# Stick-breaking scores copied to SBUF by ScalarE, and attention steps taken at one point of a weight chunk where there were two

## The chip, the cores and the metric

One NeuronCore of a Trainium2 chip runs the whole kernel. The metric is the device time of one execution in microseconds. TensorE is called PE here, its weight loads PEld, VectorE DVE, ScalarE ACT, GpSimd POOL, and the queue that issues the transfers SP.

## The reference, cut to what matters

One decoder layer over 512 tokens of width 2048. After an RMSNorm, one projection `w_in` gives the inputs of two groups of 16 heads of width 64. Group A is sliding-window attention (window 128) with four key/value heads, normalised queries and keys, a relative bias and a sink per head. Group B is stick-breaking attention, and it is this group's arithmetic that the change touches:

```python
z = jnp.einsum('bhqd,bhsd->bhqs', q_blk, kt) * scale          # scores
log_beta = jax.nn.log_sigmoid(z)
log_1m = jnp.where(causal, jax.nn.log_sigmoid(-z), 0.0)
later = lax.cumsum(log_1m, axis=3, reverse=True) - log_1m
w = jnp.where(causal, jnp.exp(log_beta + later), 0.0)         # causal: key before query
out = jnp.einsum('bhqs,bhsd->bqhd', w, vt)
```

With sp(z) = log(1 + exp(z)), the exponent is z minus the sum of sp over the keys from s up to the query. Both groups' outputs are normalised, go through one projection `w_out`, and are added to x; a squared-ReLU MLP of width 8192 follows.

## The kernel before, in words

**Projections.** All products keep float32 precision by three matmuls on split operands (a high part `hi` and a remainder `lo`). `wchunk` (L95) loads a piece of weights, 2 x 128 rows of 512 columns, and splits it: ACT casts it to `hi` (L91), DVE subtracts to get `lo` (L92). The loaded pieces have four buffers (`wst`), the `hi` and `lo` tiles four each (`whl`). A group of 512 projected columns takes 8 such chunks. A chunk is 24 matmuls of 128x512 for four accumulators `m` (or `t`) of PSUM, six for each. The groups follow one another: keys and values of A, two groups of queries of A (`qa`), values of B (`v0`), two groups of queries and keys of B (`qk0`, `qk1`), `v1`, `qk2`, `qk3`, and then the output projection of A's half (`out_group(0, n)`, four times four chunks).

**Attention inside the projections.** Attention has no stage of its own. Its steps are interleaved with the projections' chunks by `pump` (L283), which is called twice in every chunk: after the second accumulator (the middle) and after the fourth (the end). The unit of work is a piece of a pair of heads: two units (`hf`) for each of 8 pairs of A, four units (`i`, one for each block of 128 queries) for each of 8 pairs of B, 48 units in all. A unit has a `begin` and an `end`. `begin` computes the scores (tile `sc` in A, `z` in B, two PSUM banks, one for each head) and the long chain of small operations behind them. `end` transposes the finished weights on PE (tile `ptr` in A, `wtr` in B, two banks), DVE copies the transposes to SBUF (`turned`, `wt`); the last unit of a pair (in A, of two pairs) also multiplies them with the values (`av`, `bv`) and passes the result to `finish_o` (L377).

**The order by `pump`.** Its calls are counted by `clock`. On an odd call, the middle of a chunk, the next unit begins if one is due (`LAG` = 11 calls after it was enqueued). On an even call, the end of a chunk, the unit before the one that has just begun ends. The `end` of a unit therefore comes one and a half chunks after its `begin`. A `None` in the queue `flight` marks a call in which nothing began, so that the last unit can end too. The generators in `chains` (the norms of A's queries and keys) are advanced on each call. A unit's two score banks, two transpose banks and the output bank all come from the pool `pa`, which has four banks (`bank`, L86); the other four (`pp`) hold the projection's accumulators.

**The chain of a unit of B** (`weights`, L562) for each of its two heads, on 128 x w elements with w = 128, 256, 384 or 512: ACT takes the absolute value of `z` (L571), its exponential (L572) and logarithm (L573) in tile `a`; DVE adds max(z, 0) into tile `b` (L574); POOL zeroes the diagonal block's upper part (L575); DVE sums from the right with a scan into `a` (L578); DVE subtracts `a` from `z` into `b` (L580); POOL masks (L581); ACT takes the exponential (L583). L571, L574 and L580 read `z` in PSUM. Tiles `a` and `b` come from the pool `wk` with two buffers for each tag.

Instructions run in order on each engine. The framework places each engine's instructions by the order in the program and by readiness in its own model, so that a few matmuls of a projection may stand between two steps of attention.

Of the kernel before, what the change touches and what calls it, by code (L numbers as in the profile page):

```python
# [15 lines left out]
ALU = mybir.AluOpType  # L16
# [4 lines left out]
P = 128  # L21
# [37 lines left out]
def hymba_layer(ctx: ExitStack, tc: tile.TileContext, x, norm_attn_g, w_in, q_norm_g, k_norm_g,  # L59
                sinks, rel_bias, swa_out_g, sb_out_g, w_out, norm_mlp_g, w_up, w_down, sel, eye, out):  # L60
    nc = tc.nc
    x, out = x[0], out[0]
# [211 lines left out]

    chains, units, flight, clock = [], deque(), deque(), [0]

    def enqueue(pair_units):
# [3 lines left out]
    def pump():  # L283
        clock[0] += 1
        chains[:] = [g for g in chains if next(g, None) is not None]
        if clock[0] % 2:
            begun = bool(units) and units[0][0] <= clock[0]
            if begun:
                begin, end = units.popleft()[1]
                begin()  # L290
                flight.append(end)
            flight.append(None) if not begun and flight else None
        elif len(flight) > 1:
            end = flight.popleft()
            if flight[0] is None:
                flight.clear()
            end()

    def drain():
        while units or flight:  # L300
# [124 lines left out]
    def swa_pair(g, m, q, turned):  # L425
        c = 4 * g + m
        k = kT[g]
        heads = (8 * g + m, 8 * g + m + 4)
        bias = []

        def load_bias():
            bias.append(wk.tile([P, 2, 2 * P], F32, tag="bias", bufs=4, name=f"bias{c}"))

            with tc.issue_after(last_in[0].ins):
                for s in range(2):
                    nc.sync.dma_start(out=bias[0][:, s], in_=bias_ap(heads[s]))
        prs_of = {}

        def scores(hf):
            sc = [bank(f"sc{c}_{hf}{s}") for s in range(2)]  # L440
            for nn in range(2):
                n = 2 * hf + nn
                k0 = max(n - 1, 0) * P
                o0 = nn * 256 if n else P
                for a, b in ((0, 0), (0, 1), (1, 0)):
                    for s in range(2):
                        rows = slice(s * DH, (s + 1) * DH)
                        nc.tensor.matmul(sc[s][:, o0:o0 + 256], q[rows, a, n * P:(n + 1) * P],
                                         k[rows, b, k0:k0 + 256],
                                         start=(a == 0 and b == 0), stop=(a == 1))  # L450
            return sc

        def softmax(hf, sc):
            prs = []
            bt = bias[0]
            for s in range(2):
                h = heads[s]
                pr = wk.tile([P, 2, 256], F32, tag=("wa", "wb")[s], name=f"pr{c}_{hf}{s}")
                scv = sc[s].rearrange("p (n k) -> p n k", n=2)
                if hf == 0:  # L460
                    nc.gpsimd.memset(pr[:, 0, 0:P], NEG)
                    nc.vector.tensor_tensor(out=pr[:, 0, P:], in0=scv[:, 0, P:], in1=bt[:, s, P:], op=ALU.add)
                    nc.vector.tensor_tensor(out=pr[:, 1], in0=scv[:, 1], in1=bt[:, s], op=ALU.add)
                else:
                    nc.vector.tensor_tensor(out=pr, in0=scv,
                                            in1=bt[:, s:s + 1].broadcast_to([P, 2, 256]), op=ALU.add)
                mx = sm.tile([P, 2], F32, tag="mx", name=f"mx{c}_{hf}{s}")
                nc.vector.tensor_reduce(out=mx, in_=pr, axis=AX.X, op=ALU.max)
                nm = sm.tile([P, 2], F32, tag="nm", name=f"nm{c}_{hf}{s}")
                nc.vector.tensor_scalar(out=nm, in0=mx, scalar1=sink[:, h:h + 1], scalar2=-1.0,  # L470
                                        op0=ALU.max, op1=ALU.mult)
                den = sm.tile([P, 2], F32, tag="den", name=f"den{c}_{hf}{s}")
                es = sm.tile([P, 2], F32, tag="es", name=f"es{c}_{hf}{s}")
                for nn in range(2):
                    nc.scalar.activation(out=pr[:, nn], in_=pr[:, nn], func=AF.Exp, bias=nm[:, nn:nn + 1],
                                         accum_out=den[:, nn:nn + 1])
                nc.scalar.activation(out=es, in_=nm, func=AF.Exp, bias=sink[:, h:h + 1])
                nc.vector.tensor_tensor(out=den, in0=den, in1=es, op=ALU.add)
                nc.vector.reciprocal(out=den, in_=den)
                for nn in range(2):  # L480
                    nc.gpsimd.tensor_scalar(out=pr[:, nn], in0=pr[:, nn], scalar1=den[:, nn:nn + 1],
                                            scalar2=1.0, op0=ALU.mult, op1=ALU.mult)
                prs.append(pr)
            return prs

        def turn(hf, prs):
            b0 = 1 if hf == 0 else 0
            f0 = 0 if hf == 0 else 3 * P
            for s in range(2):
                tr = bank(f"ptr{c}_{hf}{s}")  # L490
                prf = prs[s].rearrange("p n k -> p (n k)")
                for b in range(b0, 4):
                    nc.tensor.transpose(tr[:, b * P:(b + 1) * P], prf[:, b * P:(b + 1) * P], ident)
                nc.vector.tensor_copy(out=turned[m][:, s, f0:f0 + (4 - b0) * P], in_=tr[:, b0 * P:])

        def begin(hf):
            if hf == 0:
                load_bias()
            prs_of[hf] = softmax(hf, scores(hf))

        def end(hf):
            if hf == 0:
                turned[m] = wtp.tile([P, 2, 7 * P], F32, tag="wt", name=f"pt{c}")
            turn(hf, prs_of.pop(hf))
            if hf == 0 or m % 2 == 0:
                return

            for s in range(2):
                kv = slice((2 * g + s) * DH, (2 * g + s + 1) * DH)
                av = bank(f"av{c}_{s}")  # L510
                for j in (0, 2, 1, 3):
                    n = min(256, T - j * P)
                    for r in range(2):
                        nc.tensor.matmul(av[r * DH:(r + 1) * DH, j * P:j * P + n], va[j][:, kv],
                                         turned[m - 1 + r][:, s, j * 256:j * 256 + n],
                                         start=(j == 0), stop=(j == 3))
                finish_o(av, 0, 4 * g + 2 * s + m // 2)

        return [(partial(begin, hf), partial(end, hf)) for hf in range(2)]
# [29 lines left out]
    def sb_pair(c, q, k, vs, keep):  # L549
# [12 lines left out]
        def weights(i, sc):  # L562
            w = (i + 1) * P
            dg = slice(i * P, (i + 1) * P)
            ws = []
            for s in range(2):
                z = sc[s][:, 0:w]
                a = wk.tile([P, 512], F32, tag=("wa", "wc")[s], name=f"a{c}_{i}{s}")[:, 0:w]
                b = wk.tile([P, 512], F32, tag=("wb", "wd")[s], name=f"b{c}_{i}{s}")[:, 0:w]

                nc.scalar.activation(out=a, in_=z, func=AF.Abs)  # L571
                nc.scalar.activation(out=a, in_=a, func=AF.Exp, scale=-1.0)  # L572
                nc.scalar.activation(out=a, in_=a, func=AF.Ln, bias=1.0)  # L573
                nc.vector.scalar_tensor_tensor(out=b, in0=z, scalar=0.0, in1=a, op0=ALU.max, op1=ALU.add)  # L574
                nc.gpsimd.affine_select(out=b[:, dg], in_=b[:, dg], pattern=[[-1, P]], compare_op=ALU.is_gt,  # L575
                                        fill=0.0, base=0, channel_multiplier=1)

                nc.vector.tensor_tensor_scan(out=a[:, ::-1], data0=ones2[:, 0:1].broadcast_to([P, w]),  # L578
                                             data1=b[:, ::-1], initial=0.0, op0=ALU.mult, op1=ALU.add)
                nc.vector.tensor_tensor(out=b, in0=z, in1=a, op=ALU.subtract)  # L580
                nc.gpsimd.affine_select(out=b[:, dg], in_=b[:, dg], pattern=[[-1, P]], compare_op=ALU.is_gt,  # L581
                                        fill=NEG, base=0, channel_multiplier=1)
                nc.scalar.activation(out=b, in_=b, func=AF.Exp)  # L583
                ws.append(b)
            return ws
# [13 lines left out]
        def end(i):  # L599
            if i == 0:  # L600
                wt.extend(wtp.tile([P, 4, 512], F32, tag="wt", name=f"wt{c}_{s}") for s in range(2))
            turn(i, ws_of.pop(i))
            if i < 3:
                return
            av = bank(f"bv{c}")
            cc = c % 4
            for j in range(4):
# [454 lines left out]
    for cj in range(2 * NC):  # L1062
# [8 lines left out]
        for s, (name, ai, _, b, more) in enumerate(d_products(cj)):  # L1071
# [36 lines left out]
            a = act[c, ai]  # L1108

            at_end = q == 14 * NC - 1  # L1110
            for h, tt in sorted(((h, tt) for h in range(2) for tt in range(2)), key=lambda x: x[::-1] if at_end else x):
# [3 lines left out]
                for kk in range(2):  # L1115
                    al, ar = a[:, 0, 2 * h + kk, ts], a[:, 1, 2 * h + kk, ts]
                    first, end = h == 0 and kk == 0 and not more, h == 1 and kk == 1
# [36 lines left out]
```

## Time and profile before

| what | us |
|---|---|
| median of 3 runs (1998.0 to 1998.86) | 1998.21 |
| the profiled execution's own time | 1998.97 |
| span of its trace, first to last instruction | 1997.2 |
| PE busy in it | 1976.4 |
| DVE busy in it | 1649.4 |
| ACT busy in it | 1037.5 |
| POOL busy in it | 1011.3 |

Matmuls are pipelined and a recorded matmul overlaps the next, so PE's busy time is close to the span almost everywhere and says little about lost time. The distance between the starts of two neighbouring projection matmuls says more: whatever stands between them shows as a longer distance. Attention of A lies between about 139 and 280 us of the span, that of B between 319 and 455 us (pairs 0 to 3) and 494 and 629 us (pairs 4 to 7).

### The profile page before, as it was taken

To read this page: it belongs to the slowest core of one execution; us is meant where nothing else is said; L and a number is where in the kernel's file an instruction comes from. 1 tells how busy PE (TensorE), PEld (TensorE's weight loads), DVE (VectorE), ACT (ScalarE), POOL (GpSimd) and SP (SyncE) were. 2 spreads that over 40 slices of the span, in tenths; PEclk is the share of its full clock that TensorE was granted. 3 is DMA by queue.
4 is the path that set the end of the run, shared out by engine and by line. 5 is a ranking of instruction groups with operands and counts; after the bars stand their busy time and mean duration, and the time that the engine had idled before them with its cause. 6 is when DMAs were issued, how large, how long until landed. Compare 5 with 4: busy or idle time off the path is not lost.

```text
span 1997.2 us, 31358 instructions
## 1 busy us (share of the span) xinstructions
PE 1976.4 (99%) x11652; PEld 1717.5 (86%) x11652; DVE 1649.4 (83%) x2142; ACT 1037.5 (52%) x1900; POOL 1011.3 (51%) x898
## 2 busy tenths in 40 slices
PE   8999999999999999999999999999999999999999
PEld 7887787778777889999999999998888888888887
DVE  4469654664776479999999999999999999999997
ACT  6357544453554575656565656565443333333444
POOL 0013431221321038777777777776866656656653
PEclk9999999999999999999999999999999999999999
DMA  6732332224245555665656565656766457456451
GB/s 224 146 119 80 100 98 83 75 69 137 93 140 172 192 169 180 217 201 189 208 181 215 180 216 181 212 176 245 290 250 250 158 221 291 161 221 261 143 204 67
DMA packets 213916, 350.31 MB, mean 175 GB/s; under 512 B 9779, under 2 KB 154372, under 8 KB 206596
## 3 DMA queue, kind: packets, MB, share of 16 engines
q1 hardware_dynamic: 211216, 345.02, 51.0%
q10 hardware_dynamic: 2548, 3.30, 1.3%
q8 instruction: 91, 1.49, 0.3%
q14 instruction: 61, 0.50, 0.1%
HBM read 270.16 MB, written 78.12 MB: 174 GB/s over the span
## 4 chain that ended last, share of the span: by engine, by line
PE 89%; DVE 5%; ACT 3%; POOL 1%; issue 1%; DMA 1%; POOLq 0%; SPq 0%; DVEq 0%; ACTq 0%
PE ps_u L831 11%; PE ps_u L830 11%; PE ps_u L832 11%; PE ps_d L1119 9%; PE ps_d L1120 9%; PE ps_d L1118 9%; PE ps_qk L123 3%; PE ps_qk L125 3%; PE ps_qk L124 3%; PE ps_o L125 2%; PE ps_o L123 2%; PE ps_o L124 2%; PE ps_qa L123 1%; PE ps_qa L124 1%; PE ps_qa L125 1%; DVE lo_d L92 1%
## 5 line engine op out<-in xcount | busy, mean ns | idle before, releaser
L832 PE MATMUL ps_u<-h2h,lo_u 128*128 128x256 f32 x1792 | 507.5, 283 | 0.1
L830 PE MATMUL ps_u<-h2h,hi_u 128*128 128x256 f32 x1792 | 507.6, 283 | 0.0
L831 PE MATMUL ps_u<-h2l,hi_u 128*128 128x256 f32 x1792 | 507.4, 283 | 0.0
L1118 PE MATMUL ps_d<-hi_d,ad 128*128 128x512 f32 x896 | 348.8, 389 | 2.7 <-ACT e L856 2.7
L1119 PE MATMUL ps_d<-lo_d,ad 128*128 128x512 f32 x896 | 349.0, 390 | 0.1
L1120 PE MATMUL ps_d<-hi_d,ad 128*128 128x512 f32 x896 | 348.7, 389 | 0.0
L832 PEld LDWEIGHTS ps_u<-h2h,lo_u 128*128 128x128 f32 x1792 | 344.1, 192 | 0.3 <-DVE lo_u L92 0.3
L831 PEld LDWEIGHTS ps_u<-h2l,hi_u 128*128 128x128 f32 x1792 | 344.2, 192 | 0.0
L830 PEld LDWEIGHTS ps_u<-h2h,hi_u 128*128 128x128 f32 x1792 | 344.1, 192 | 0.0
L806 POOL TENSOR_TENSOR s_u<-st_u 128x256 f32<-128x256 f32 x256 | 212.1, 849 | 245.1 <-DVE lo_u L92 176.3
L965 POOL TENSOR_TENSOR T<-st_d,T 128x1024 f32<-128x1024 f32 x64 | 174.2, 2724 | 188.3 <-DVE lo_d L92 185.8
L92 DVE TENSOR_TENSOR lo_d<-T,hi_d 128x1024 fp32r<-128x1024 f32 x128 | 250.5, 1971 | 19.5 <-ACT hi_d L91 18.9
L92 DVE TENSOR_TENSOR lo_u<-s_u,hi_u 128x512 fp32r<-128x512 f32 x256 | 261.8, 1023 | 0.3 <-ACT hi_u L91 0.3
L91 ACT CAST hi_u<-st_u 128x384 fp32r<-128x384 f32 x256 | 131.2, 513 | 229.4 <-PE ps_u L831 224.1
L91 ACT CAST hi_d<-T 128x1024 fp32r<-128x1024 f32 x128 | 134.9, 1055 | 188.5 <-PE ps_d L1120 175.6
L92 DVE TENSOR_TENSOR lo_u<-st_u,hi_u 128x384 fp32r<-128x384 f32 x256 | 196.1, 766 | 30.4 <-ACT hi_u L91 29.5
L1118 PEld LDWEIGHTS ps_d<-hi_d,ad 128*128 128x128 f32 x896 | 168.2, 188 | 38.0 <-ACT e L856 3.1
L1119 PEld LDWEIGHTS ps_d<-lo_d,ad 128*128 128x128 f32 x896 | 168.2, 188 | 36.1 <-DVE lo_d L92 1.3
L1120 PEld LDWEIGHTS ps_d<-hi_d,ad 128*128 128x128 f32 x896 | 168.2, 188 | 34.8
L92 DVE TENSOR_TENSOR lo_d<-st_d,hi_d 128x1024 fp32r<-128x1024 f32 x96 | 189.7, 1988 | 9.1 <-ACT hi_d L91 9.0
L91 ACT CAST hi_d<-st_d 128x1024 fp32r<-128x1024 f32 x96 | 101.3, 1056 | 154.3 <-PE ps_d L1120 135.4
L91 ACT CAST hi_u<-s_u 128x512 fp32r<-128x512 f32 x256 | 158.5, 619 | 18.0 <-POOL s_u L806 18.0
(242 smaller groups left out, 3818.9 us busy)
## 6 DMA issues: line engine op xcount, KB each, us to landing
st_u<-in_w_up SPq DMA_DIRECT2D x128, 512.0 KB, 3.7
st_d<-in_w_down SPq DMA_DIRECT2D x64, 1024.0 KB, 8.3
ad<-ac SPq DMA_DIRECT2D x56, 1024.0 KB, 6.3
ac<-ah SPq DMA_DIRECT2D x32, 896.0 KB, 4.0
ac<-al SPq DMA_DIRECT2D x32, 896.0 KB, 5.8
st_qk<-in_w_in SPq DMA_DIRECT2D x64, 256.0 KB, 3.0
st_o<-in_w_out SPq DMA_DIRECT2D x32, 512.0 KB, 4.2
st_qa<-in_w_in SPq DMA_DIRECT2D x16, 512.0 KB, 4.0
```

What stands on the lines that cost most here:

```text
L91: cast = nc.scalar.copy(out=hi, in_=st)
L92: nc.vector.tensor_tensor(out=lo, in0=st, in1=hi.bitcast(F32), op=ALU.subtract)
L123: nc.tensor.matmul(ps, ah, bh, start=first, stop=False)
L124: nc.tensor.matmul(ps, ah, bl, start=False, stop=False)
L806: last_sum[0] = nc.gpsimd.tensor_tensor(out=o, in0=a, in1=b, op=op)
L830: nc.tensor.matmul(o, wh[:, a], hh[:, b], start=first, stop=False, skip_group_check=True)
L831: nc.tensor.matmul(o, wh[:, a], hl[:, b], start=False, stop=False, skip_group_check=True)
L832: nc.tensor.matmul(o, wl[:, a], hh[:, b], start=False, stop=(k == KP - 1), skip_group_check=True)
L965: nc.gpsimd.tensor_tensor(out=o, in0=raw[cj, a, h], in1=raw[cj, b, h], op=ALU.subtract)
L1118: nc.tensor.matmul(o, al, bh[:, kk], start=first, stop=False, skip_group_check=True)
L1119: nc.tensor.matmul(o, al, bl[:, kk], start=False, stop=False, skip_group_check=True)
L1120: nc.tensor.matmul(o, ar, bh[:, kk], start=False, stop=end, skip_group_check=True)
```

## The change

In `weights`, ACT first copies the scores `z` to tile `b` in SBUF; the sum with max(z, 0), the mask and the scan then work in place in tile `a`, and the last subtraction takes the scores from `b`. In `pump`, the `end` of a unit moves from the end of a chunk to the middle of the next one, in front of the `begin` that stands there; its product with the values is split off as `values` and comes behind that `begin`. The marker `None` goes. Even calls now only advance `chains`.

```diff
         if clock[0] % 2:
             begun = bool(units) and units[0][0] <= clock[0]
+            values = flight.popleft()() if len(flight) > 1 or flight and not begun else None
             if begun:
                 begin, end = units.popleft()[1]
                 begin()
                 flight.append(end)
-            flight.append(None) if not begun and flight else None
-        elif len(flight) > 1:
-            end = flight.popleft()
-            if flight[0] is None:
-                flight.clear()
-            end()
+            if values:
+                values()
...
             turn(hf, prs_of.pop(hf))
-            if hf == 0 or m % 2 == 0:
-                return
+            return values if hf and m % 2 else None
+
+        def values():
...
+                nc.scalar.copy(out=b, in_=z)
 
                 nc.scalar.activation(out=a, in_=z, func=AF.Abs)
                 nc.scalar.activation(out=a, in_=a, func=AF.Exp, scale=-1.0)
                 nc.scalar.activation(out=a, in_=a, func=AF.Ln, bias=1.0)
-                nc.vector.scalar_tensor_tensor(out=b, in0=z, scalar=0.0, in1=a, op0=ALU.max, op1=ALU.add)
-                nc.gpsimd.affine_select(out=b[:, dg], in_=b[:, dg], pattern=[[-1, P]], compare_op=ALU.is_gt,
+                nc.vector.scalar_tensor_tensor(out=a, in0=z, scalar=0.0, in1=a, op0=ALU.max, op1=ALU.add)
+                nc.gpsimd.affine_select(out=a[:, dg], in_=a[:, dg], pattern=[[-1, P]], compare_op=ALU.is_gt,
                                         fill=0.0, base=0, channel_multiplier=1)
 
                 nc.vector.tensor_tensor_scan(out=a[:, ::-1], data0=ones2[:, 0:1].broadcast_to([P, w]),
-                                             data1=b[:, ::-1], initial=0.0, op0=ALU.mult, op1=ALU.add)
-                nc.vector.tensor_tensor(out=b, in0=z, in1=a, op=ALU.subtract)
+                                             data1=a[:, ::-1], initial=0.0, op0=ALU.mult, op1=ALU.add)
+                nc.vector.tensor_tensor(out=b, in0=b, in1=a, op=ALU.subtract)
...
             turn(i, ws_of.pop(i))
-            if i < 3:
-                return
+            return values if i == 3 else None
+
+        def values():
```

## Rows read from the trace of the kernel before

**Rows 1.** The page: the chain that ended last, shares of the span by engine.

```profile
PE 89%; DVE 5%; ACT 3%; POOL 1%; issue 1%; DMA 1%; POOLq 0%; SPq 0%; DVEq 0%; ACTq 0%
```

**Rows 2.** Windows: start:end, length, PE, PEld, DVE, ACT, POOL busy, clock, DMA.

```profile
319.00:455.00 136.00, 132.38 (x648) 98.99 (x647) 89.18 (x150) 73.72 (x161) 33.77 (x70) 0.99 0.25 73
455.00:494.00 39.00, 39.00 (x174) 32.28 (x173) 15.19 (x16) 13.19 (x17) 7.32 (x5) 1.00 0.44 138
```

**Rows 3.** Waits of PEld, 130 to 660 us: total us, times, longest.

```profile
PEld z L558 <- DVE b L580: 9.8, 18, 1.1
PEld bv L609 <- DVE wt L593: 6.2, 16, 0.5
...
PEld wtr L592 <- ACT b L583: 1.5, 2, 1.0
```

**Rows 4.** Timeline of PE at narrow scores: start us, us; brackets: idle before.

```profile
361.86 0.39 PE L125 MATMUL ps_v<-hi_v,hT 128*128 128x512 f32 x1
...
362.73 0.51 PE L123 MATMUL ps_v<-hi_v,hT 128*128 128x512 f32 x1
363.07 0.40 PE L124 MATMUL ps_v<-lo_v,hT 128*128 128x512 f32 x1
...
382.58 0.39 PE L125 MATMUL ps_v<-hi_v,hT 128*128 128x512 f32 x1
383.61 1.21 PE L558 MATMUL z<-hl_b,hl_b 64*128 64x256 f32 x6 [0.64 <-DVE b L580]
384.75 0.50 PE L123 MATMUL ps_v<-hi_v,hT 128*128 128x512 f32 x1
...
588.69 0.39 PE L125 MATMUL ps_o<-hi_o,ohl 128*128 128x512 f32 x1
...
590.77 0.50 PE L123 MATMUL ps_o<-hi_o,ohl 128*128 128x512 f32 x1
```

**Rows 5.** Timeline of PE, matmuls around the 512-wide scores.

```profile
339.63 0.39 PE L125 MATMUL ps_v<-hi_v,hT 128*128 128x512 f32 x1
...
343.27 0.79 PE L123 MATMUL ps_v<-hi_v,hT 128*128 128x512 f32 x1
...
375.21 0.39 PE L125 MATMUL ps_v<-hi_v,hT 128*128 128x512 f32 x1
...
376.55 0.50 PE L123 MATMUL ps_v<-hi_v,hT 128*128 128x512 f32 x1
...
514.14 0.39 PE L125 MATMUL ps_o<-hi_o,ohl 128*128 128x512 f32 x1
...
517.22 0.50 PE L123 MATMUL ps_o<-hi_o,ohl 128*128 128x512 f32 x1
```

**Rows 6.** Window behind the first of those scores, columns as in rows 2.

```profile
344.00:348.00 4.00, 4.00 (x19) 3.26 (x18) 0.93 (x2) 2.94 (x6) 1.57 (x2) 0.79 0.48 135
```

**Rows 7.** Timeline of PE around a unit's eight transposes.

```profile
387.37 0.40 PE L125 MATMUL ps_v<-hi_v,hT 128*128 128x512 f32 x1
387.61 1.04 PE L592 MATMUL wtr<-ident,b 128*128 128x128 f32 x8
388.40 0.48 PE L123 MATMUL ps_v<-hi_v,hT 128*128 128x512 f32 x1
```

**Rows 8.** Timeline of DVE, the chain of a 512-wide unit.

```profile
379.21 1.29 DVE L574 SCALAR_TENSOR_TENSOR b<-z,a 128x512 f32<-128x512 f32 x2 [1.80 <-ACT a L573]
...
382.89 1.26 DVE L580 TENSOR_TENSOR b<-z,a 128x512 f32<-128x512 f32 x2
```

**Rows 9.** Timeline of ACT, the same unit.

```profile
376.54 1.09 ACT L571 ACTIVATE a<-z 128x512 f32<-128x512 f32 x2
...
384.70 0.62 ACT L583 ACTIVATE b<-b 128x512 f32<-128x512 f32 x1
```

**Rows 10.** Tile z: count, min/median/max ns, first and last start.

```profile
L571 ACT ACTIVATE a<-z x64: 257/432/599, 320.9 to 615.7; 128x128 f32<-128x128 f32 x16, 128x256 f32<-128x256 f32 x16, 128x384 f32<-128x384 f32 x16, 128x512 f32<-128x512 f32 x16
```

**Rows 11.** Timeline of POOL, the same unit's first masks.

```profile
380.03 0.29 POOL L575 TENSOR_SCALAR_AFFINE_SELECT b<-b 128x128 f32<-128x128 f32 x1 [4.00 <-DVE b L574]
380.63 1.09 POOL L575 TENSOR_SCALAR_AFFINE_SELECT b<-b 128x128 f32<-128x128 f32 x1 [0.30 <-DVE b L574]
```

## The prediction

> **What bounds the kernel now.** I read the chain that ended last first: it runs through PE for 89% of the span [rows 1], so the time is PE's work plus what PE waits for. The change touches only the stretch in which attention is interleaved with projections, so next come the windows of that stretch. Without attention PE places 173 or 174 matmuls in 39.00 us, one every 0.23 us. In the first stretch of group B the same matmuls share 136 us with attention, and there DVE is busy for 89.18 us and ACT for 73.72 us [rows 2]. Neither of the two is full; ACT has some 62 us to spare. PE is the bound in this stretch too, and the question is only which waits stand in its queue.
>
> The list of what the weight loads waited for answers that. The scores of B wait 9.8 us for the subtraction L580, the product with the values 6.2 us for the copies of the transposes, and the transposes 1.5 us for the last exponential [rows 3]. A weight load runs ahead of its matmul, so part of each wait is hidden. The true price is seen in the distance between the projection matmuls on both sides. Around a narrow score that waits for nothing it is 362.73 - 361.86 = 0.87 us. Around the score that follows a 512-wide unit it is 384.75 - 382.58 = 2.17 us and, at the last such place, 590.77 - 588.69 = 2.08 us [rows 4]. There are four such places, each 1.2 to 1.3 us too long. The releaser in the row is L580 because a score needs two of the four banks, and the unit before still holds its two until L580 has read `z`.
>
> Around a 512-wide score that waits for nothing the distance is 376.55 - 375.21 = 1.34 us. At the first pair of each half of B it is 343.27 - 339.63 = 3.64 us and 517.22 - 514.14 = 3.08 us [rows 5], 2.30 and 1.74 us too long. After the first of these PE's granted clock averages 0.79 over 4 us [rows 6], which loses another 0.21 x 4 = 0.84 us: between its two levels of 2.4 and 1.2 GHz it spent part of the window at the lower, after PE had stood idle.
>
> **The change part by part.**
>
> *The bank is given back earlier.* `z` is now read last by L574. For a 512-wide unit L574 ends at 380.50 us where L580 ends at 384.15 us [rows 8], 3.65 us earlier. The two copies come in front and cost as much as the two absolute values of the same size, 1.09 us [rows 9]. So the banks come free about 2.6 us earlier, at 381.6 us, while the next score was wanted soon after 382.58 us [rows 4]; now it has the transposes of another unit in front of it as well, which for a 512-wide unit take 388.40 - 387.37 - 0.23 = 0.80 us [rows 7]. The four waits go: 4 x 1.25 = **-5.0 us**, all of it PE's own time.
>
> *The first wide score of each half.* Here DVE and ACT also evacuate the projected queries and keys, and everything is late. The same 2.6 us stand against 2.30 and 1.74 us, so both could go, with the low clock: -4.88 us at most. But ACT has 4 copies more in just these chunks. If one of the two waits stays, -1.7 remains. I take **-4.0**.
>
> *Transposes half a chunk later.* The end of a unit moves by 12 matmuls, 2.8 us; the chain gets 1.09 us longer. The 1.5 us of waits for the last exponential go: **-1.5** (bounds -1.5 and 0).
>
> *Values behind the next score.* The copies of the transposes used to be covered by what the framework put in between; now a score stands there, at least 0.64 us of PE work (0.87 - 0.23). The 6.2 us are the upper bound, 0 the lower, since some waits may be hidden already and DVE can be at a cast when the transposes end. I take **-2.0**, nearer to the lower end because a score is shorter than the two copies.
>
> *Fewer interruptions.* The matmul behind a score is followed at 363.07 - 362.73 = 0.34 us in place of 0.23 [rows 4], so a return to the projection costs 0.11. Transposes and scores now come together in all 48 units: up to 48 x 0.11 = 5.3 us less, or nothing if the step from transposes to scores costs the same. I take **-1.0**.
>
> *Added work on ACT.* 64 copies from PSUM, sizes as in L571, 64 x 432 ns = 27.6 us [rows 10] over the two stretches of B, 14 us each against some 62 us free in the first [rows 2]. Queued behind them on ACT are the casts of weights, for which DVE's `lo` and then PE wait; with four buffers those run chunks ahead, and no projection matmul stands in the list of waits for them. Priced at nothing for that cover. If it were gone, every copy would be PE's loss, 27.6 us.
>
> *Latency of the chain.* This is the point to watch, since transposes that come too early block everything behind them on PE. For the wide unit the scores start at 375.44 us (375.21 + 0.23) and the last exponential ends at 385.32 [rows 5, 9], 9.9 us; with the copies 11.0. After the change the transposes come 48 matmuls (11.0 us), two scores (1.11 + 0.64) and one set of transposes (at most 0.80) later: 13 to 13.5 us. Two and more us of room. Against this speaks POOL: its first mask takes 0.29 us and the second 1.09 us [rows 11], which ends only as the first head's scan on DVE does. The subtraction now has both inputs in SBUF, so it may do the same to a mask: at most 0.7 us for each unit, inside the room, so the sum doesn't move.
>
> The Trainium skill (SBUF — State Buffer, "Who interferes with whom") says that a VectorE instruction with two SBUF inputs contends with a GpSimd instruction that reads SBUF, and one with at most one SBUF input does not. The long mask agrees with it; the subtraction leaves the harmless class by this change. By the rule 32 units x 0.7 us would be 22 us of chain, and none of PE's time as long as the room holds.
>
> *Moved issues and buffers.* The `end` takes with it 14 writes of outputs by SP, half a chunk later; SP's weight loads are queued behind each. Those run ahead by the four staging buffers, so nothing. Two units are now in flight all the time, so in group A the squares of the query norm find both buffers of their tag taken until the next transposes: half a chunk, 2.8 us, once, off PE's path unless the norm's matmul is placed too early. With the values' place among DVE's casts I allow **+1.5** for new waits (0 to 6). The last unit ends 2.8 us later, still inside the output projection, and nothing after it waits.
>
> Sum: -5.0 - 4.0 - 1.5 - 2.0 - 1.0 + 1.5 = -12.0 us against the profiled execution's 1998.97 us (span 1997.2 and 1.8 around it). That execution lies 0.76 us above the median, so for the median 1998.21 - 12.0 = **1986.2 us**.
>
> **The rivals.**
>
> *The waits only move.* The bank is free, but the framework places transposes and values earlier to fit, and the time returns as waits for the copies (6.2 us already there) or for the exponential. For it: every wait listed in [rows 3] is one the framework's own order did not foresee. Against it: four places with one cause and 2.6 us of slack gained against 1.3 us of wait. Then some 2 to 4 us are left: about **1996**. Chance 0.17.
>
> *Everything goes at once*: -5.0 - 4.9 - 1.5 - 6.2 - 4.3 = -22, **1976**. For it: the return and the copies have rows with their price. Against it: a score is too short to cover both copies. Chance 0.10.
>
> *The chain becomes late (slower).* If the chain of the wide units grows by more than the 2 us of room, through copies that queue behind casts on ACT, its transposes wait and hold up scores and values behind them. It decides from a chain of about 13.5 us on. 16 units are 384 or 512 wide; 2 us on each is +32, less the 12 gained: about **2018**. For it: at the first pair the wide score starts at 339.9 and its chain was late already. Against it: in the steady units the chain is done in 9.9 us. Chance 0.13.
>
> **How the numbers follow.** The forecast has 0.60, with a range of its own of 1980 to 1992. I call a difference of more than 0.2%, 4 us, measurable here. Faster than 1994.2: 0.60 + 0.10 + a third of the first rival, 0.75. Within: the rest of it and a little of the third, 0.13. Slower: 0.12. The range of 8 in 10 leaves out most of the large gain and the late chain: 1979 to 2000.
>
> **What would show it.** In the trace after: no wait of `z` for L580, and none for L574 in its place; distances around scores near 0.87 and 1.34 us; the granted clock at 1.00 behind the first wide scores; ACT's copies in its idle time; bv's waits under 6.2 us; the stretches of B shorter by 4 to 6 us each and that of A about the same. The prediction is wrong if transposes wait for exponentials, if values wait for copies longer than before, or if the MLP's part changes its length.

## The result, and the profile after

The changed kernel takes **2011.97 us** (median of 6 runs, 2009.48 to 2014.0) against 1998.11 for the kernel before beside it: ratio **1.0069** (95% interval 1.0056 to 1.0082), 13.9 us slower. The forecast was 1986.2, 12.0 us faster. The sign was wrong, and the time lies outside the range.

The chain that ended last still runs through PE for 89% (compare [rows 1]), so here too the loss is sought between PE's matmuls. The same windows as in [rows 2], and the one of [rows 6], in the kernel after:

```profile
319.00:455.00 136.00, 129.07 (x614) 99.08 (x613) 87.90 (x146) 84.22 (x189) 28.71 (x69) 0.96 0.23 72
455.00:494.00 39.00, 38.21 (x176) 30.63 (x175) 16.71 (x18) 12.77 (x17) 8.46 (x6) 1.00 0.41 128
...
344.00:348.00 4.00, 2.52 (x15) 1.95 (x14) 1.97 (x3) 3.97 (x10) 0.70 (x2) 1.00 0.39 124
```

In the first stretch of group B PE places 614 matmuls where it placed 648. ACT is busy for 10.5 us more and still idle for 52, PE stands idle for 6.9 us instead of 3.6, and the mean clock is 0.96 instead of 0.99. The waits of the weight loads, as in [rows 3]:

```profile
PEld z L557 <- DVE a L574: 17.7, 11, 2.4
...
PEld bv L610 <- DVE wt L593: 2.6, 9, 0.4
```

The wait of the scores for their banks, which was to go, grew from 9.8 to 17.7 us; the values' wait fell from 6.2 to 2.6. One place of it on PE, the score behind the 512-wide unit, where [rows 4] show 0.64 us of idle time:

```profile
379.95 0.39 PE L125 MATMUL ps_v<-hi_v,hT 128*128 128x512 f32 x1
380.18 0.82 PE L592 MATMUL wtr<-ident,b 128*128 128x128 f32 x6
380.92 0.61 PE L557 MATMUL z<-hl_b,hl_b 64*128 64x256 f32 x3
...
384.64 0.62 PE L557 MATMUL z<-hl_b,hl_b 64*128 64x256 f32 x3 [1.98 <-DVE a L574]
...
386.04 0.63 PE L124 MATMUL ps_v<-lo_v,hT 128*128 128x512 f32 x1
386.47 0.63 PE L125 MATMUL ps_v<-hi_v,hT 128*128 128x512 f32 x1
```

Three of the six matmuls, those of the first head, go at 380.92; the other three wait until 384.64 for the second head's L574. Shortly behind the wait the projection's matmuls start 0.43 us apart instead of 0.23. Over 386 to 389 us the granted clock is 0.50, the 1.2 GHz level:

```profile
386.00:389.00 3.00, 3.00 (x8) 2.30 (x7) 2.67 (x9) 1.21 (x3) 0.79 (x3) 0.50 0.12 41
```

Why is the second head late? Follow DVE and ACT through this unit, first DVE (compare [rows 8], where both sums stand in one row that starts at 379.21):

```profile
379.90 0.69 DVE L574 SCALAR_TENSOR_TENSOR a<-z,a 128x512 f32<-128x512 f32 x1 [3.34 <-ACT a L573]
381.05 1.23 DVE L578 TENSOR_TENSOR_SCAN a<-ones,a 128x512 f32<-128x512 f32 x1 [0.46 <-POOL a L575]
382.19 1.20 DVE L92 TENSOR_TENSOR lo_qk<-st_qk,hi_qk 128x1024 fp32r<-128x1024 f32 x1
383.30 0.68 DVE L580 TENSOR_TENSOR b<-b,a 128x512 f32<-128x512 f32 x1
383.90 0.69 DVE L574 SCALAR_TENSOR_TENSOR a<-z,a 128x512 f32<-128x512 f32 x1
```

and ACT (compare [rows 9]):

```profile
376.35 0.53 ACT L583 ACTIVATE b<-b 128x384 f32<-128x384 f32 x1 [2.29 <-POOL b L581]
376.78 0.57 ACT L569 COPY b<-z 128x512 f32<-128x512 f32 x1
...
379.21 0.65 ACT L573 ACTIVATE a<-a 128x512 f32<-128x512 f32 x1
379.73 0.65 ACT L572 ACTIVATE a<-a 128x512 f32<-128x512 f32 x1
380.25 1.06 ACT L91 CAST hi_qk<-st_qk 128x1024 fp32r<-128x1024 f32 x1
381.19 0.66 ACT L573 ACTIVATE a<-a 128x512 f32<-128x512 f32 x1
...
389.37 1.03 ACT L583 ACTIVATE b<-b 128x512 f32<-128x512 f32 x3
```

The 512-wide scores run on PE from 373.70 to 374.67, but ACT takes the first copy at 376.78. In front of it in ACT's queue stands the last exponential of the unit before (128x384), which waits 2.29 us for its mask. That mask waits for DVE:

```profile
376.02 0.29 POOL L581 TENSOR_SCALAR_AFFINE_SELECT b<-b 128x128 f32<-128x128 f32 x1 [2.52 <-DVE b L580]
```

Then the heads run staggered instead of side by side. The second head's logarithm comes behind a cast and ends at 381.85, and on DVE its sum comes behind the first head's scan, a cast and the first head's subtraction. Its bank is free at 384.59, where the forecast had 381.6. From first score to last exponential the unit takes some 16 us instead of 9.9 (the ACT row at 389.37 holds this unit's second exponential and two short ones of the next unit).

Where the 14.0 us of span went: the first matmul of the MLP's up projection starts at 744.04 instead of 732.55 us, 11.5 us later. To see where these 11.5 us arise, follow the same projection matmuls, counted from the first, through both kernels. The one that starts at 139.92 us before starts at 139.64 after the change, that of 319.07 at 316.73, that of 494.09 at 498.33, and the last, of 732.32, at 743.81. So the stretch of group A gains 2.1 us, and the two of B lose 6.6 and 7.2. Of these 13.8 us, 6.7 are steps between neighbouring projection matmuls with nothing in between that are stretched by over 0.15 us: 39 of them (8.3 us) where there were 6 (1.6), matmuls at the low clock.

The other 2.5 us come later, for the most part at the start of the MLP's down projection. PE waits there for 2.8 us, before for 2.7; but the 6 us from about its end on go at a granted clock of 0.50 after the change, at 1.00 before. After the change, and before:

```profile
1400.00:1406.00 6.00, 5.55 (x13) 4.43 (x14) 6.00 (x7) 5.12 (x11) 3.59 (x2) 0.50 1.02 426
```

```profile
1388.00:1394.00 6.00, 5.64 (x25) 4.72 (x26) 6.00 (x7) 5.09 (x10) 3.54 (x2) 1.00 1.01 425
```

The experiments below show the same: where the trace has no low clock in the first 30 us of the down projection (before, e7, e16, e18), the part from the up projection to the end takes 1264.7 to 1265.6 us; where it has some 7 us of it (the change, e2, e5, e6, e15), 1267.2 to 1268.3. Why the clock falls there in some kernels and not in others is not shown; the change alters nothing in that part.

### The profile page after: what moved, and what is told of

It reads as the page before. It is cut to its first block, busy times and chain, and to the rows that moved or that the text cites. A ratio compares the mean times of both kernels' runs of the same rounds, so it can differ in the third digit from the quotient of the medians.

```text
span 2011.2 us, 31474 instructions
## 1 busy us (share of the span) xinstructions
PE 1980.6 (98%) x11652; PEld 1727.9 (86%) x11652; DVE 1657.3 (82%) x2142; ACT 1062.0 (53%) x1964; POOL 1001.7 (50%) x898
## 3 DMA queue, kind: packets, MB, share of 16 engines
q8 instruction: 91, 1.49, 0.3%
## 4 chain that ended last, share of the span: by engine, by line
PE 89%; DVE 4%; ACT 3%; issue 1%; POOL 1%; DMA 1%; POOLq 0%; SPq 0%; DVEq 0%; ACTq 0%
PE ps_u L832 10%; PE ps_u L831 10%; PE ps_u L833 10%; PE ps_d L1119 10%; PE ps_d L1120 10%; PE ps_d L1121 10%; PE ps_qk L123 2%; PE ps_qk L125 2%; PE ps_qk L124 2%; PE ps_o L125 2%; PE ps_o L123 2%; PE ps_o L124 2%; PE ps_qa L123 1%; PE ps_qa L125 1%; PE ps_qa L124 1%
```

## The experiments

Eighteen kernels were run. Times are medians, ratios are to the kernel before, run beside each. In the table "steps" is the change's order in `pump`, "together" means that each operation of the chain is written for both heads before the next one, and "bound" that a unit's last exponentials are bound behind the next unit's logarithms on ACT.

| run | steps | copies | heads | exponentials | us | ratio (95%) |
|---|---|---|---|---|---|---|
| the change | new | yes | apart | free | 2011.97 | 1.0069 (1.0056, 1.0082) |
| e1 | new | no | apart | free | 2003.2 | 1.0021 (1.0011, 1.0032) |
| e2 | old | yes | apart | free | 2022.09 | 1.0116 (1.0101, 1.0131) |
| e5 | old | unread | apart | free | 2018.9 | 1.0096 (1.008, 1.0113) |
| e11 | old | off the chain | apart | free | 2009.67 | 1.0052 (1.0035, 1.0069) |
| e3 | new | sum reads it | apart | free | 2019.51 | 1.0101 (1.0086, 1.0116) |
| e6 | new | behind Ln | apart | free | 2012.01 | 1.0069 (1.0053, 1.0085) |
| e4 | new | yes | together | free | 2009.55 | 1.0053 (1.0038, 1.0068) |
| e10 | new | yes, no first Exp | apart | free | 2004.4 | 1.0026 (1.0017, 1.0036) |
| e12 | new | yes, short chain | apart | free | 2003.09 | 1.0026 (1.0016, 1.0035) |
| e7 | new | yes | apart | written later | 2012.98 | 1.0069 (1.0054, 1.0084) |
| e8 | new | sum reads it | together | written later | 2011.1 | 1.0057 (1.0042, 1.0072) |
| e9 | new | sum reads it | together | bound | 1990.16 | 0.9954 (0.9939, 0.9969) |
| e13 | new | yes | apart | half bound | 2001.84 | 1.0009 (1.0, 1.0018) |
| e18 | new | yes | apart | bound | 1993.89 | 0.9972 (0.996, 0.9985) |
| e15 | new | yes | together | bound | 1989.68 | 0.9949 (0.9934, 0.9964) |
| e14 | new | no | together | bound | 1998.25 | 0.9996 (0.9987, 1.0006) |
| e17 | old | yes | together | bound | 2001.87 | 1.0014 (1.0004, 1.0023) |
| e16 | new | yes, short chain | together | bound | 1986.39 | 0.9937 (0.992, 0.9953) |

**The two halves.** e1 is the diff's `pump` and `values` alone, e2 its `weights` alone.

> The new order of the steps (end, begin, values in the middle of a chunk), but no copy: the scores stay in PSUM until the subtraction, as before. Theory 1 (a bank held too long by the second head's sum L574, which the copies pushed behind the first head's scan): the copies are to blame, so without them the waits are those for the subtraction as before, some 1 to 2 us at each of 7 pairs: 1993 to 2003 us. Theory 2 (the new order is to blame whatever the chain looks like): 2007 to 2015 us. Theory 3 (ACT has too much work): under 1998 us.

> The copies and the sums in place, but the old order of the steps, twice in a chunk. Theory 1: the second head's sum is late here too, and the next score waits for it: 2000 to 2012 us, with waits of z for L574 in the trace. Theory 2: 1990 to 1999 us. Theory 3: 2005 to 2015 us, with waits for the exponential or for hi and lo, not for L574.

Each half is slower by itself, the copies by far more (23 us against 4). With the new steps alone the scores wait for the subtraction 12.6 us where it was 9.8:

```profile
PEld z L557 <- DVE b L579: 12.6, 14, 1.7
```

With the copies alone, in the old order of steps, the transposes wait for the last exponential:

```profile
PE wtr L593 <- ACT b L584: 19.4, 12, 3.3
```

So the copies make the chain late, and the new order hides part of that.

**Is it the bank?** e3 lets the sum read the copy, so that neither head's L574 holds a bank.

```diff
-                nc.vector.scalar_tensor_tensor(out=a, in0=z, scalar=0.0, in1=a, op0=ALU.max, op1=ALU.add)
+                nc.vector.scalar_tensor_tensor(out=a, in0=b, scalar=0.0, in1=a, op0=ALU.max, op1=ALU.add)
```

> The changed kernel with one operand changed: the sum L574 reads the copy b in place of z, so the banks are given back after ACT's absolute values, some 4 to 5 us earlier for the second head. The work on every engine stays. Theory 1: the waits of z (13.6 us on PE) go, and with them the stretches at the lower clock (about 6.7 us): 1986 to 1995 us, granted clock 1.00 in both stretches of B. Theories 2 and 3: 2005 to 2015 us.

The largest wait of the change went, and the ratio rose from 1.0069 to 1.0101, another 6 us. The wait reappeared further down the chain:

```profile
PE wtr L592 <- ACT b L583: 9.3, 6, 2.4
PE bv L610 <- DVE wt L593: 6.8, 5, 1.6
```

The loss shows at the bank, but an earlier bank alone does not cure it.

**Heads together.** e4 writes each operation for both heads (`zs`, `aa`, `bb` hold the two heads' tiles):

```diff
-            for s in range(2):
...
-                nc.scalar.copy(out=b, in_=z)
-
-                nc.scalar.activation(out=a, in_=z, func=AF.Abs)
+            for z, b in zip(zs, bb):
+                nc.scalar.copy(out=b, in_=z)
+            for z, a in zip(zs, aa):
+                nc.scalar.activation(out=a, in_=z, func=AF.Abs)
...
```

> The changed kernel with the chain written operation by operation for both heads, so that both sums L574 stand in front of both scans on DVE; z is still read by the sum. Theory 1: the second head's sum ends about 2 to 3 us earlier, most of the waits go: 1986 to 1998 us. Theories 2 and 3: 2005 to 2015 us.

The interval overlaps that of the change. The scores' wait on PE fell from 13.6 to 3.9 us and the values' rose to 10.5. Again the wait only moved.

**Copies that do nothing.** e5 adds a copy to the kernel before, in front of L571, that is overwritten unread; e11 puts an unread copy behind the last exponential.

```diff
+                nc.scalar.copy(out=b, in_=z)
                 nc.scalar.activation(out=a, in_=z, func=AF.Abs)
```

```diff
                 nc.scalar.activation(out=b, in_=b, func=AF.Exp)
+                nc.scalar.copy(out=a, in_=b)
```

> The kernel before, with the copy of z into b by ACT added in front and nothing else: b is overwritten by the sum as before, and nobody reads the copy. Theory 4 (the units' chains run one behind the other through ACT's queue, since a unit's exponential stands in front of the next unit's first operation; the copies lengthen each chain and push the second head behind the first head's scan): the loss is ACT's alone, so about that of the copies with the old order, 2012 to 2024 us, with waits of wtr for the exponential. Theory 5 (the data's way matters: sums in place, a subtraction with both inputs in SBUF): 1998 to 2004 us.

> The kernel before with an unread copy on ACT of the same size, placed behind the last exponential (b into a), where no step of its own unit waits for it. The same 64 copies as in e5, only not in front of the chain. Theory 6 (chain length): 1996 to 2006 us. Theory 3 (27 us more time on ACT): 2012 to 2024 us, as in e5.

A copy that nobody reads costs 19 us in front of the chain and 10 behind it. In the changed kernel ACT is idle for over a third of the first stretch of B with the same number of copies, which speaks for the place in the queue as the price, and not the work.

**Where the copy stands, and how long the chain is.** e6 moves the copy behind the logarithm. e10 drops the first exponential (L572); e12 takes exp(z) and ln(1 + exp(z)) directly, without L571 and L574.

```diff
-                nc.scalar.copy(out=b, in_=z)
...
                 nc.scalar.activation(out=a, in_=a, func=AF.Ln, bias=1.0)
+                nc.scalar.copy(out=b, in_=z)
```

```diff
-                nc.scalar.activation(out=a, in_=z, func=AF.Abs)
-                nc.scalar.activation(out=a, in_=a, func=AF.Exp, scale=-1.0)
+                nc.scalar.activation(out=a, in_=z, func=AF.Exp)
                 nc.scalar.activation(out=a, in_=a, func=AF.Ln, bias=1.0)
-                nc.vector.scalar_tensor_tensor(out=a, in0=z, scalar=0.0, in1=a, op0=ALU.max, op1=ALU.add)
```

> The changed kernel with the copy moved behind the logarithm on ACT: the same work, but no longer in front of the chain. Theory 4: the heads stay closer together and the chain is up to 1 us shorter, so part of the loss goes: 1994 to 2006 us. Theory 3 (27 us more work on ACT is what costs): 2008 to 2014 us as in the changed kernel.

> The changed kernel without the exponential of minus the absolute value (L572), which is left out, so the weights are other numbers; its time on ACT and in the chain is about that of the copy, so that both are again what they were before the copies. Theory 6 (what costs is 1 to 2 us more of chain for each unit, wherever the framework then lets PE meet it): 1996 to 2005 us, like the new order alone. If the copies cost through something else: over 2007 us.

> The changed kernel with log(1 + exp(z)) taken directly by two ACT operations: no absolute value, no sum with max(z, 0) on DVE. The copies stay; ACT's work is about that before, DVE does 64 sums less (about 29 us), the chain of a wide unit is some 2 us shorter, and z is last read by ACT. Theory 6: bank and chain are early, 1980 to 1994 us. If neither bank nor chain sets the waits: over 2000 us.

The copy's place within the chain makes no difference (e6). Taking one operation of the copy's size off ACT (e10) gives back 8 to 9 us, and taking DVE's sum off as well (e12) gives no more. e12 also misses the 1980 to 1994 us that a shorter chain and an earlier bank were to give: neither is enough by itself. What e10 and e12 share is one ACT operation less in each chain, which points at ACT; these runs cannot tell ACT's time from its order.

**The order on ACT.** e7 writes a unit's last exponentials in the program behind the next unit's first logarithm; e8 does so with heads together and the sum from the copy. e9 is e8 with that order made binding:

```diff
-            for a in aa:
-                nc.scalar.activation(out=a, in_=a, func=AF.Ln, bias=1.0)
-            tail()
+            for a in aa:
+                ln = nc.scalar.activation(out=a, in_=a, func=AF.Ln, bias=1.0)
+            with tc.issue_after(ln.ins):
+                tail()
```

`tail()` issues the exponentials that were put aside in `tails`.

> The changed kernel with the last exponentials of a unit issued behind the next unit's first logarithm, so that on ACT no unit waits for the one before. Nothing else moves. Theory 4: the chains overlap, the waits of z for the sum L574 shrink: 1986 to 2002 us. Theory 3: 2008 to 2016 us. Against it: an exponential that comes later can make the transposes wait.

> The changed kernel with both heads in step, the sum reading the copy b, and the exponentials behind the next unit's logarithms. Theory 4: bank and chain are both early, PE waits for neither: 1982 to 1992 us, granted clock 1.00. Theory 3: over 2005 us, since ACT does the same 64 copies.

> The kernel of e8 (heads in step, sum reads the copy, exponentials issued behind the next unit's logarithms) with that order on ACT made binding; in e8 the framework still placed them in front of the next unit's copies, and ACT stood 2.9 us before them. Theory 4 (each unit's chain waits for the one before through ACT's queue): a wide unit's chain starts 2 us earlier, the waits of bv and wtr go: 1984 to 1998 us. If the chain's own length is what is too long, not the queue in front of it: 2004 to 2014 us.

Written later alone changed nothing (e7 and e8 both miss what they were expected to give), because the framework put them in front again. ACT in e8, around the 512-wide unit's copies:

```profile
375.65 0.52 ACT L552 ACTIVATE b<-b 128x384 f32<-128x384 f32 x1 [2.90 <-POOL b L590]
376.88 0.53 ACT L552 ACTIVATE b<-b 128x384 f32<-128x384 f32 x1 [0.70 <-POOL b L590]
377.31 1.06 ACT L574 COPY b<-z 128x512 f32<-128x512 f32 x2
```

and in e9, where the copies wait for PE's scores alone:

```profile
372.07 1.08 ACT L574 COPY b<-z 128x512 f32<-128x512 f32 x2 [2.18 <-PE z L563]
...
376.08 0.95 ACT L552 ACTIVATE b<-b 128x384 f32<-128x384 f32 x2
```

With the same 64 copies e9 is 21 us faster than e8 and faster than the kernel before. The rival that the price is ACT's added 27 us of work falls here.

**What of e9 is needed.** e13 and e18 put the binding into the change itself, heads apart, sum from the bank. In e13, other than its expectation says, the first head's exponential is bound only behind its own second head's logarithm; e18 binds both behind the next unit's:

```diff
+                ln = nc.scalar.activation(out=a, in_=a, func=AF.Ln, bias=1.0)
+                if s == 1:
+                    with tc.issue_after(ln.ins):
+                        while tails and tails[0][:2] != (c, i):
+                            tail(tails[0][:2])
```

(e13 has a plain `tail()` there.) e15 is e9 with the sum from the bank, e14 is e9 without copies (sum and difference from the bank), e17 is e15 with the old order of steps, e16 is e9 with the short chain of e12.

> The changed kernel with one rule added: a unit's last two exponentials come on ACT behind the next unit's two logarithms, and that order is binding. Copies, in-place sums, heads one after the other and the sum that reads the bank are as in the changed kernel. If the one edge on ACT (a unit's last exponentials in front of the next unit's copies) is the whole cause, this run is near 1990 to 1994. If it takes the heads side by side and the early release of the bank as well, it stays at 2003 to 2010, with the scores' bank wait on the second head's sum as the largest wait. If the edge is nothing by itself, 2010 to 2014.

> The changed kernel and the bound order alone, as it was meant: in the run before it of this kind the first head's exponential was bound only behind its own second head's logarithm; here both exponentials of a unit come behind the second logarithm of the next unit, binding. Heads are still written one after the other and the sum reads the bank. If the one edge on ACT carries the loss, 1988 to 1993, near the kernel with heads side by side (ratio 0.995). If the heads side by side are needed as well, it stays near the half-bound one, 1998 to 2003 (ratio 1.000).

> The kernel of the bound order with heads side by side and copies, but the sum reads the bank and only the difference reads the copy, as in the change. If the bank is what the order freed, the wait of the scores on the sum comes back with 3 to 6 us and the time is 1993 to 1998. If the bank does not matter once the order is bound, 1988 to 1992.

> The kernel of the bound order with heads side by side, but without the 64 copies: the sum and the difference read the bank, the sum goes to a tile of its own. If the copies are what gives the gain (early bank), this is slower than the bound kernel with copies by 5 to 10, 1995 to 2000. If the copies give nothing and the order gives all, it is at 1984 to 1990, that or faster than with copies, since 28 us of ACT are saved.

> The kernel of the bound order with heads side by side, copies and the sum from the bank, but with the order of the attention's steps as before (transposes behind the next unit's scores, values in the same step). If the change's order of the steps is a gain once ACT's order is bound, this is slower by 3 to 8, 1994 to 1999. If that order gave its gain only together with the copies of the unbound kernel, or gives nothing, 1987 to 1991. If it costs what it cost alone (4 of the first run), 1983 to 1987.

> The kernel of the bound order with heads side by side and copies, with the weights' first half shortened: exp(z) and ln(1 + exp) in place of abs, exp, ln and the sum on DVE. If the rest of the loss is still the length of a unit's chain (values behind weights, 6.4 us of waits left), the values' wait falls to under 3 and the time is 1982 to 1987. If the chain no longer bounds once the order is bound, 1988 to 1991.

The binding alone takes the change from 1.0069 to 0.9972, some 19 us (e18); e13, half bound, lies between. Heads together give a little more (0.9949), though the intervals of e18 and e15 touch. With the order bound, the sum may read the bank at no loss (e15 against e9).

e14 and e17 take one half of the change away again. Against e15 the copies are worth 9 us and the new steps 13. Without the copies the binding does far less: from e1 to e14, which also puts the heads together, the ratio falls from 1.0021 to 0.9996, 5 us. The binding in the kernel before, with neither copies nor new steps, was not run, so what it is worth there is not shown. Without the copies the scores wait until the subtraction lets go of the bank, here e14:

```profile
PEld z L563 <- DVE b L589: 10.6, 16, 2.1
```

and with the old steps the transposes and values come too early for the longer chain, here e17:

```profile
PEld bv L621 <- DVE wt L605: 12.4, 15, 1.7
PEld wtr L604 <- ACT b L553: 10.0, 27, 1.1
```

The short chain (e16) has the lowest time measured, 1986.39 us, but its interval overlaps that of e15.

## Why the prediction was wrong

**The step that failed is the cost of the copies on ACT.** "Priced at nothing for that cover" named the wrong cover. I looked at what the copies might delay among PE's projections, the casts of weights, and that was harmless: no projection matmul appears among the large waits. But ACT's queue also orders the units against each other. What ACT waited for over 319 to 629 us, first in the kernel before, the lines of the last exponential and of the first operation on the scores:

```profile
ACT b L583 <- POOL b L581: 52.9, 28, 3.7
ACT a L571 <- PE z L558: 26.4, 15, 2.4
```

after the change,

```profile
ACT b L583 <- POOL b L581: 62.4, 40, 3.3
ACT b L569 <- PE z L557: 23.1, 15, 2.7
```

and in e15, where the exponentials' wait for their masks is nearly gone:

```profile
ACT b L574 <- PE z L563: 52.7, 29, 3.1
...
ACT b L552 <- POOL b L591: 7.7, 8, 2.9
```

Of the "62 us to spare" of [rows 2], the 26.7 us of this line of the kernel before, over 319 to 455 us, were the largest piece:

```profile
ACT b L583 <- POOL b L581: 26.7, 14, 3.4
```

ACT stood at an exponential whose mask had not come, with the next unit's work queued behind it. In the kernel before this cost little at the unit shown: [rows 9] have the first absolute value at 376.54, when its scores had only just been made. With the new steps the same scores are there 2.1 us before ACT turns to them. Idle time of an engine whose queue is blocked is not free time; that the wait stood in the trace of before, as the largest of ACT's, shows that it could have been read. That this order, and not the work of the copies, is the price is shown by e18: with the same copies it is 19 us faster than the change.

**"Latency of the chain"** was right for the order it assumed and wrong for the order that came. The prediction added the copies to a chain that starts with its scores. The forecast was 11.0 us for the wide unit. In e15, where nothing of the unit before stands in front and the heads go side by side, it runs from 370.35 to 381.33, 10.98 us:

```profile
370.35 0.97 PE L563 MATMUL z<-hl_b,hl_b 64*128 64x512 f32 x6
```

```profile
371.40 1.08 ACT L574 COPY b<-z 128x512 f32<-128x512 f32 x2 [2.18 <-PE z L563]
...
380.18 1.15 ACT L552 ACTIVATE b<-b 128x512 f32<-128x512 f32 x2 [0.34 <-POOL b L591]
```

In the changed kernel it took some 16 us, past the 13.5 from which the third rival decided.

**"The bank is given back earlier"** (-5.0): the first head's L574 ends at 380.59, earlier than the forecast 381.6; the second's at 384.59. I had read the pair as one row and taken for granted that they stay a pair. In e15 the term came true: the scores wait 1.9 us for DVE in all, never over 0.2 us.

**The first wide scores** (-4.0): these two waits went as forecast (compare [rows 5]), but new ones came behind them:

```profile
337.52 0.98 PE L557 MATMUL z<-hl_b,hl_b 64*128 64x512 f32 x6
...
346.32 0.61 PE L557 MATMUL z<-hl_b,hl_b 64*128 64x256 f32 x3 [1.49 <-DVE a L574]
...
350.32 0.62 PE L557 MATMUL z<-hl_b,hl_b 64*128 64x256 f32 x3 [1.81 <-DVE a L574]
```

The wide score of the first pair has no wait; the narrow ones behind it wait 1.49 and 1.81 us, and in the second half of B 1.10 and 1.81 us, each for a second head's L574. The term also read the old waits only in part: in the kernel before, 0.77 us of each of the two waits ended with DVE's copies of transposes and not with L580, here the first:

```profile
341.94 1.40 PE L558 MATMUL z<-hl_b,hl_b 64*128 64x512 f32 x5 [0.77 <-DVE wt L593]
```

That these waits went does therefore not follow from an earlier bank alone; here the term was in part lucky. **The transposes** (-1.5): 1.0 us of their waits on PEld is left of 1.5, a third of the term. **The values** (-2.0) went the way forecast in the change, from 6.2 to 2.6 us, and not in e15, where they wait 8.5: with the scores on time they are the next to be late. **Fewer interruptions** (-1.0) was too low: group A, where the order of steps is all that changes, gained 2.1 us, and the other runs with the new steps agree (2.0 to 2.2; those with the old steps less than 0.1). Whether all of that is fewer returns to the projection is not shown.

**The rivals.** The third, on the slow side (2018, chance 0.13), had the mechanism, copies and casts in ACT's queue, but not the place: it expected waiting transposes. Those came in e2 and e3; in the change itself the second head's bank was the first to be late. The first rival, that waits only move, has the mechanism of e3, e4 and e8, though not their time: it still expected a gain of 2 to 4 us. In the second, the interruptions stand with 4.3 us where their own bound is 5.3, which changes its 1976 by 1 us.

**The sum itself** came close only with another order. With the order on ACT bound and the heads together, e15 measured 0.9949 of 1998.21, 10.2 us less, against the 12.0 forecast. That is in part luck, since the terms do not all agree with it: the values wait longer there and group A gains more. What the forecast lacked was the question whether the new instructions take the places in the queue that the sum assumes.

**The masks.** I left out of the sum a longer mask through the subtraction's two SBUF inputs, with 0.7 us for each unit as a bound. The 64 masks behind it (L581) took 19.7 us before, 24.5 in the change and 32.5 in e15; e14, with the order of e15 and a subtraction that still reads the bank, has 22.7. The direction agrees with the rule of the Trainium skill (SBUF — State Buffer, "Who interferes with whom"), that a VectorE instruction with two SBUF inputs contends with a GpSimd instruction that reads SBUF. The growth stays under the 22 us of the bound, and e15 is the faster kernel with the longer masks, so they don't carry the loss. The masks behind the sum (L575) took 33.1, 20.5 and 38.2 us; they differ with what DVE happens to do beside them.

**Open.** Why the framework puts the exponentials in front and staggers the heads when copies are added stays open; the runs show only that it does so and what it costs. The prediction named a change of the MLP's length as a sign of being wrong; the 2.5 us found there go with the clock at the start of the down projection, and why that differs stays open.

## What to carry to other kernels

An engine that is half idle may still be the bound of a chain: look at what it was standing at while idle, and what was queued behind that, before an instruction on it is priced at nothing. When a stage works on several units at once, check that on the engine they share no unit's last step stands in front of the next unit's first; here that one order was worth some 19 us, and only with it were the copies worth anything. And when removing the largest wait makes another grow by as much, stop moving waits and look for the chain that feeds them all.

## What the runs showed of the hardware

Some of PE's waits cost more than their length. After the wait of 1.98 us shown above, PE ran at the 1.2 GHz level from about 386 to 389 us, eight steps of 0.39 to 0.43 us for 0.23, 1.6 us on top of the wait; after the 0.64 us of [rows 4] the clock of the next 2.6 us was 1.00. The length of the wait does not decide it alone: in the change a wait of 1.37 us that ended at 600.25 was followed by a mean clock of 0.66 over 5 us and one of 1.34 us that ended at 567.20 by 1.00, and in e2 two waits of 2.64 us, which ended at 578.11 and 612.34, were followed by 1.00. The prediction had priced such a loss once, at [rows 6], and not in its allowance for new waits. It made up about half of what the stretches of B lost.

The price of 64 added copies on ACT, some 27 us of work, depended on the order in its queue: 64 unread ones cost 19 us in front of the chain (e5) and 10 us behind it (e11), while with the order bound the kernel with copies is 9 us faster than the one without (e15 against e14).
